# Rounded w_down blocks moved from w_up into w_o, and a new order of the first w_up products

## The chip, the cores and the metric

The kernel runs on one core of a Trainium2 chip. The metric is the device time of one execution in microseconds (us), the median of three runs. One execution was also taken with the hardware profiler; the profile's times are counted from the first instruction of that execution.

## The reference, cut to what matters

One encoder layer on 512 tokens of width 2048, all in float32: an attention and pooling part that ends in the product with `w_o`, a normalised residual, and a feed-forward part that ends in the product with `w_down`.

```python
m = concat(a, p) @ w_o                       # (512, 2048) @ (2048, 2048)
x = x + rms_norm(m, post_mix_g)
h = rms_norm(x, pre_ffn_g)
up = causal_dwconv(h @ w_up, conv_w, conv_b) # w_up: (2048, 2 * 5632), three taps along the tokens
y = (gelu(up[..., :5632]) * up[..., 5632:]) @ w_down
x = x + rms_norm(y, post_ffn_g)
```

## The kernel before, in words

**Arithmetic.** A float32 operand is split into a rounded part and the rest: ScalarE writes the rounded part (`L141`), VectorE subtracts it from the source (`L142`). A product is then rounded x rounded + rounded x rest + rest x rounded. The large products use a scheme with seven instead of eight half-size products (numbered 1 to 7), in which some factors are sums of blocks. Product 1 needs the weight block (0,0); the sums of products 5, 6 and 4 are made one from another, by adding further blocks to the same tile with a DMA that accumulates. Such DMAs are issued on GpSimd (`L1087` for w_up). Products 3 and 7 share a second tile in the same way, product 2 has a block of its own.

**Stages.** The order is: q, k, v and pooling projections and attention (to about 390 us), w_o with its seven products (to 548 us), the passage to w_up, w_up in 43 pairs of column blocks with seven products each and one plain block beforehand (to 1456 us), w_down in chunks, and the output.

**Order.** TensorE's instructions run in the order in which the program writes them. For the other engines a planner orders the instructions by estimated times, within the dependencies; each engine and each DMA queue (SP's and GpSimd's) then works its list in order, so that an instruction that waits holds everything listed behind it. A tile takes its place in memory when it is first used, in the group of buffers that its tag names, and gives it back after its last use.

**w_o.** `wo_product(i, cc)` runs one product on one column half, in four steps of one weight tile each. A step takes a tile that was loaded and rounded ahead (four tiles ahead rounded, two more loaded).

**The passage.** The last w_o product ends with tokens 256 to 511 not yet normalised. `norm`, `x2`, `keep_x` and `norm_x` make the new residual, and `hn` is its normalised form. `turn_back(2, pair, ...)` turns two of the sixteen column blocks of `hn` on TensorE (tile `xt`); ScalarE copies them out (`L989`), and after every second pair a quarter of `hT` (tile `gT`) is rounded. Eight such turns are needed. Products 1 and 2 need only tokens 0 to 255 and can run before them. The plain block (`up`, in four quarters, weights `w_0` to `w_3`) needs the turned tokens, and the other products need the sums of h that `h_sums` makes on VectorE and ScalarE (tiles `a` and `h`).

**w_up.** `Factors` holds the order of all products, loads raw weights ahead, and rounds them ahead: `get()` hands out the next and calls `prefetch`, which loads up to ten entries and rounds up to four ahead. Rounded weights lie in eight buffers (`w4`, two for each weight), raw ones in five (`raw4`) and in four more (`raw_x`). Pairs in `alone` use block (0,0) by itself for product 1 and load a new tile for the sum of product 5. The order starts with

```python
begin = [(k, i) for k in range(3) for i in (1, 2)] + [(0, 5), (3, 1), (0, 3), (3, 2), (0, 6)]
self.order[6:6] = [("w", q) for q in range(4)]
```

where `(k, i)` is product i of pair k and `("w", q)` a quarter of the plain block. Results of products 1, 6, 7 and 4 of one pair add up in one PSUM bank (`qa`), 5 and 3 in another (`qg`), 2 in a third (`qd`); `keep` copies them out.

**w_down's first chunk.** Its factors are prepared earlier. Sums of blocks are written to DRAM tiles `t5`, `t7`, `t6`, `t4` (`first_sum`), one step at a time, by `more_sums(1)`: a copy (`L302`, or `L305` on SP's queue late in the kernel) or an accumulation (`L309`, GpSimd). Three factors that need no sum (`READY`) are rounded ahead as six half blocks (`ready_parts`): each is loaded to `rw`, rounded to `rwh` and `rwl`, and both are stored to DRAM. Before the change these six stand as entries `(None, at)` in w_up's order, from entry 60 on, every 24 entries.

Of the kernel before, what the change touches and what calls it, by code (L numbers as in the profile page):

```python
# [9 lines left out]
F32 = mybir.dt.float32  # L10
# [5 lines left out]
P = 128  # L16
# [16 lines left out]
AHEAD = 3  # L33
READY_FROM, READY_EVERY = 60, 24
SCALE = 1.0 / math.sqrt(DH)
# [47 lines left out]
def encoder_layer(ctx: ExitStack, tc: tile.TileContext, x, xT, vecs, rel, post_mix, post_ffn,  # L83
# [121 lines left out]
    def g_tokens(gT, kb, t):  # L205
        return tuple(v[:, t % 2 * P:(t % 2 + 1) * P] for v in g_half(gT, kb, t // 2))

    def part(w, *idx):
        return tuple(v[(slice(None),) + idx] for v in w)
# [78 lines left out]

    first_sum = {i: [dram.tile([P, CU, S], F32, name=f"t{i}{cc}") for cc in range(2)] for i in (5, 7, 6, 4)}

    def sums_in_dram():
# [322 lines left out]
    with tc.tile_pool(name="p1", bufs=2, reuse_waits="tile") as p1:  # L614
# [215 lines left out]
        def wo_left(name, k, t, tiles=None):  # L830
# [7 lines left out]
            return parts  # L838

        wo_banks = [bank(f"m{n}") for n in range(8)]  # L840
        ONTO = 6, 3, 7, 4

        def wo_product(i, cc, left, between=None):
            at = 2 * cc + (4 if i in (2, 5, 3) else 0)
            ps = wo_banks[at:at + 2]
            for q in range(4):
                w = weights.get(f"wo{i}_{cc}_{q}")
                for j in range(2):
                    kb = 2 * q + j
                    for t in range(2):  # L850
                        mm3(ps[t], tuple(v[:, kb, t * P:(t + 1) * P] for v in left), part(w, j),
                            i not in ONTO and kb == 0, kb == 7, i in ONTO)
                if between:
                    between(q)
            return ps
# [18 lines left out]
    if True:  # L874
# [161 lines left out]
        class Factors:  # L1036
# [3 lines left out]
            def __init__(self):  # L1040
# [19 lines left out]
            def load(self, k, i):  # L1060
# [7 lines left out]
                if k is None:  # L1068
                    at, j = ready_parts[i]
                    v = self.raw[k, i] = raw4("rw")  # L1070
                    nc.sync.dma_start(v.rearrange("p (a b) -> p a b", a=2),
                                      first_block(at[0], at[1] - 1, 0)[:, 2 * j:2 * j + 2, :])
                elif i == 1 and (k, "w") not in self.raw:
                    raw("w" if k in self.alone else "x", raw4("wx") if k in self.alone[:4] else raw_x("wx"), 0, 0)
                elif i == 5 and k in self.alone[:4]:
                    raw("x", raw_x("wx") if k else raw4("wx"), 0, 0)
                    self.add(k, "x", 1, 0)
# [11 lines left out]
            def make(self, k, i):  # L1089
                if k == "w":  # L1090
                    weights.tiles.append(weights.made(*weights.loaded[len(weights.tiles)]))
                    self.made.append(None)
                    return
                if k is None:
                    at, j = ready_parts[i]
                    parts = w4("rwh"), w4("rwl")
                    split(*parts, self.raw[k, i])
                    for dest, v in zip(ready_w[at], parts):
                        nc.sync.dma_start(dest[:, 2 * j:2 * j + 2, :], f32(v).rearrange("p (a b) -> p a b", a=2))
                    self.made.append(None)  # L1100
                    return
# [24 lines left out]

            def get(self, n=AHEAD):
                while self.order[self.used][0] is None:
                    self.used += 1
# [93 lines left out]
    def first_right(cc, i, ring):  # L1223

        v = ring(f"t{i}")
        source = first_sum[i][cc] if i in first_sum else first_block(cc, *{2: (1, 0), 3: (1, 1)}[i])
# [66 lines left out]
    if True:  # L1293
# [6 lines left out]

        def parts_of(v, *sizes):

            ends = [sum(sizes[:i + 1]) for i in range(len(sizes))]
            return [v[:, e - n:e] for e, n in zip(ends, sizes)]

        held = {}

        def holder(name):
# [4 lines left out]
            return held[name]  # L1313

        def two(v):
            return v.rearrange("p (a b) -> p a b", a=2)

# [164 lines left out]
        gates[0] = gate(0, plain_z(ups))  # L1482
# [8 lines left out]

        for k, i in [at for at in factors.order[10:] if at[0] is not None]:
            seven(k, i)
# [261 lines left out]
```

## Time and profile before

| | us |
|---|---|
| median of 3 runs | 1902.74 |
| lowest and highest run | 1897.75, 1904.64 |
| the profiled execution | 1895.72 |
| its span, first to last instruction | 1893.8 |
| TensorE busy in the span | 1851.8 |
| TensorE busy in 412 to 548.2 (most of w_o) | 136.20 of 136.20 |
| TensorE busy in 550 to 700 | 127.75 of 150 |
| TensorE busy in 676.7 to 1456.2 (w_up) | 772.03 of 779.5 |

A row of a timeline gives the start, the duration, engine, line, operation, the tiles written and read, the shape and the count, and in brackets the idle time before it with what ended it. Matmuls of a row overlap: the distance between starts is what counts. A row of stages gives busy time for each engine, then the clock granted to TensorE (1.00 is full), the DMA engines' mean busy share and the rate in GB/s.

### The profile page before, as it was taken

What the parts mean: (1) busy time and instruction counts of PE and PEld (TensorE: products, weight loads), DVE (VectorE), ACT (ScalarE), POOL (GpSimd) and SP (SyncE); (2) the same over time, 40 slices, a digit from 0 to 9 for tenths busy, and PEclk for the clock granted to TensorE, in tenths of its full rate; (3) what the DMA queues carried; (4) which work ended last, traced back from release to release, by engine and by line L of the source; (5) the groups of instructions that cost most, each with busy time, mean ns of one, the idle gap of its engine ahead of it and who ended that gap; (6) DMA issues with size and microseconds to landing.
All of it is one profiled execution on the core that took longest, in us unless ns stands there. A gap on an engine that the chain in (4) does not pass through costs nothing.

```text
span 1893.8 us, 25400 instructions
## 1 busy us (share of the span) xinstructions
PE 1851.8 (98%) x9530; PEld 1586.0 (84%) x9530; DVE 1489.4 (79%) x1782; ACT 1105.6 (58%) x1449; POOL 310.1 (16%) x411
## 2 busy tenths in 40 slices
PE   9999999999997899999999999999999999999998
PEld 7888888888886788888888888888888788888886
DVE  6988778787676677877777877777776799899885
ACT  7655555465585556666656566665654665565553
POOL 3411001100001121221211221212121001111111
PEclk9999999999998999999999999999999999999999
DMA  8699987997687889999989998888888977877785
GB/s 315 179 317 298 311 248 222 272 266 250 220 294 188 186 188 208 230 231 225 206 217 224 222 217 202 200 203 205 206 176 251 357 236 179 210 199 171 177 232 156
DMA packets 139610, 430.73 MB, mean 227 GB/s; under 512 B 12064, under 2 KB 15520, under 8 KB 133792
## 3 DMA queue, kind: packets, MB, share of 16 engines
q0 software_dynamic: 56016, 177.75, 46.7%
q1 hardware_dynamic: 83472, 251.36, 37.9%
q8 instruction: 75, 1.23, 0.3%
q14 instruction: 47, 0.39, 0.1%
HBM read 375.07 MB, written 104.33 MB: 253 GB/s over the span
## 4 chain that ended last, share of the span: by engine, by line
PE 87%; DMA 6%; DVE 3%; issue 2%; ACT 1%; POOL 0%; SPq 0%; POOLq 0%; DVEq 0%; ACTq 0%
PE qa L171 16%; PE qa L177 9%; PE qg L171 8%; PE qg L177 4%; PE qd L171 4%; PE pa L163 4%; PE pa L165 4%; PE pa L166 4%; PE m L163 3%; PE m L166 3%; PE m L165 3%; PE qd L177 2%; PE pg L163 2%; PE pg L165 2%; PE pg L166 2%
## 5 line engine op out<-in xcount | busy, mean ns | idle before, releaser
L171 PE MATMUL qa<-gT,wfh 128*128 128x512 f32 x1200 | 302.1, 394 | 0.0
L142 DVE TENSOR_TENSOR wfl<-x,wfh 128x1024 fp32r<-128x1024 f32 x165 | 202.0, 1224 | 91.6 <-ACT wfh L141 83.4
L171 PEld LDWEIGHTS qa<-gT,wfh 128*128 128x128 f32 x1200 | 216.7, 190 | 39.0
L141 ACT ACTIVATE wfh<-x 128x1024 fp32r<-128x1024 f32 x165 | 174.4, 1057 | 111.0 <-PE qg L171 44.3
L1087 POOL DMA_DIRECT2D x<-in_w_up x125 | 107.5, 860 | 489.6 <-DVE wfl L142 459.8
L171 PE MATMUL qg<-h,wfh 128*128 128x512 f32 x688 | 174.1, 396 | 9.1 <-ACT m L1410 9.1
L177 PE MATMUL qa<-gT,wfl 128*128 128x256 f32 x1200 | 168.5, 283 | 10.3 <-ACT m L1415 7.6
L177 PEld LDWEIGHTS qa<-gT,wfl 128*128 128x128 f32 x1200 | 157.8, 191 | 16.6 <-ACT m L1415 9.2
L171 PEld LDWEIGHTS qg<-h,wfh 128*128 128x128 f32 x688 | 130.6, 191 | 38.9 <-ACT m L1410 11.9
L142 DVE TENSOR_TENSOR bl<-b,bh 128x2048 fp32r<-128x2048 f32 x56 | 127.2, 2287 | 18.6 <-ACT bh L141 11.7
L141 ACT ACTIVATE wfh<-wy 128x1024 fp32r<-128x1024 f32 x100 | 105.3, 1053 | 60.8 <-PE qd L171 39.9
L141 ACT ACTIVATE bh<-b 128x2048 fp32r<-128x2048 f32 x56 | 106.1, 1914 | 55.9 <-DVE b L1217 23.3
L142 DVE TENSOR_TENSOR wfl<-wy,wfh 128x1024 fp32r<-128x1024 f32 x100 | 121.9, 1219 | 13.5 <-ACT wfh L141 9.2
L163 PE MATMUL pa<-bh,ah 128*128 128x512 f32 x320 | 124.5, 389 | 0.0
L165 PE MATMUL pa<-bl,ah 128*128 128x512 f32 x320 | 124.5, 389 | 0.0
L166 PE MATMUL pa<-bh,al 128*128 128x512 f32 x320 | 124.5, 389 | 0.0
L177 PEld LDWEIGHTS qg<-h,wfl 128*128 128x128 f32 x688 | 95.0, 193 | 6.9
L171 PE MATMUL qd<-gT,wfh 128*128 128x512 f32 x400 | 99.6, 391 | 0.0
L177 PE MATMUL qg<-h,wfl 128*128 128x256 f32 x688 | 96.8, 284 | 0.0
L171 PEld LDWEIGHTS qd<-gT,wfh 128*128 128x128 f32 x400 | 75.3, 189 | 15.4
L171 PE MATMUL qa<-h,wfh 128*128 128x512 f32 x344 | 86.1, 392 | 0.0
L142 DVE TENSOR_TENSOR wfl<-wz,wfh 128x1024 fp32r<-128x1024 f32 x50 | 61.2, 1223 | 28.4 <-PE qa L171 22.4
(568 smaller groups left out, 4276.4 us busy)
## 6 DMA issues: line engine op xcount, KB each, us to landing
x<-in_w_up POOLq DMA_DIRECT2D x125, 512.0 KB, 6.5
b<-in_w_down SPq DMA_DIRECT2D x32, 1024.0 KB, 6.9
wt<-in_w_o POOLq DMA_DIRECT2D x24, 1024.0 KB, 15.3
wz<-in_w_up SPq DMA_DIRECT2D x43, 512.0 KB, 5.1
wy<-in_w_up SPq DMA_DIRECT2D x43, 512.0 KB, 4.7
x<-in_w_up SPq DMA_DIRECT2D x43, 512.0 KB, 5.4
wy<-in_w_up POOLq DMA_DIRECT2D x43, 512.0 KB, 6.5
sum<-part POOLq DMA_DIRECT2D x38, 512.0 KB, 7.0
```

Of the source, the lines that this page charges most:

```text
L141: rounded = nc.scalar.activation(hi, src, AF.Copy)
L142: rest = nc.vector.tensor_sub(lo, src, f32(hi))
L163: nc.tensor.matmul(ps, l[0], r[0], start=first, stop=False, skip_group_check=onto)
L165: nc.tensor.matmul(low, l[0], r[1], start=False, stop=False, skip_group_check=onto)
L166: nc.tensor.matmul(ps, l[1], r[0], start=False, stop=last, skip_group_check=onto)
L171: nc.tensor.matmul(ps, w[0][:, kb], pairs[kb][0], start=fresh and not kb, stop=last, skip_group_check=not fresh)
L177: nc.tensor.matmul(ps[:, sl], w[1][:, kb], pair[:, sl], start=False, stop=last, skip_group_check=not fresh)
L1087: nc.gpsimd.dma_start(self.raw[k, what], self.block(k, m, kh), accum_op=ALU.add)
```

## The change

- **Pair 0 is no longer in `alone`.** Its product-1 weight tile stays; the next block is added to it after its rounding, and product 5 uses it, without a load of its own.
- **The order begins** with products 1 and 2 of four pairs; the plain block's quarters follow, then (0,5) and (0,3). Of the eight turns, 0 and 1 come after the seventh product, 2 and 3 after the eighth, 4 and 5 after the plain block's first quarter, 6 and 7 after its second.
- **Run-ahead.** Up to that point three weights are rounded ahead instead of four, and twelve entries may be loaded instead of ten; the plain block's quarters run 2, 2, 3 and 4 ahead.
- **`t4` is no longer stored.** Its copies and accumulations, which `more_sums(1)` issued at four of the turns, are gone. When w_down's first chunk needs it, `first_right` loads `t6` and adds the block with an accumulating DMA on GpSimd.
- **The six rounded half blocks** are no longer in w_up's order. `ready_step`, called after each step of w_o's products other than product 1, loads block b in step 5b, rounds it in step 5b + 5 and stores it in step 5b + 6. They use the places `h5` and `h2` in turn instead of `raw4` and `w4`; the rest is written over the raw block. `y21`, declared earlier and first written after product 4, has the place `h2` too.

```diff
-    first_sum = {i: [...] for i in (5, 7, 6, 4)}
+    first_sum = {i: [...] for i in (5, 7, 6)}
...
-                            (add, 7, (0, 1)), (add, 6, (1, 1)), (copy, 4, 6), (add, 4, (1, 0))):
+                            (add, 7, (0, 1)), (add, 6, (1, 1))):
...
+        def ready_step():
+
+            n, step[0] = step[0], step[0] + 1
+            for b, (at, j) in enumerate(ready_parts):
+                begin = 5 * b
+                if n == begin:
+                    v, hi = parts_of(h8((5, 2)[b % 2], "rw"), 1024, 1024)
+                    ready_tiles[b] = v, hi.bitcast(F32R)
+                    nc.sync.dma_start(two(v), first_block(at[0], at[1] - 1, 0)[:, 2 * j:2 * j + 2, :])
+                elif n == begin + 5:
+                    v, hi = ready_tiles[b]
+                    split(hi, v.bitcast(F32R), v)
+                elif n == begin + 6:
+                    v, hi = ready_tiles.pop(b)
+                    for dest, part_ in zip(ready_w[at], (f32(hi), v)):
+                        nc.sync.dma_start(dest[:, 2 * j:2 * j + 2, :], two(part_))
...
+                if i != 1:
+                    ready_step()
...
-                self.alone, self.open = (0, 1, 2, 3, n - 1), False
+                self.alone, self.open = (1, 2, 3, n - 1), False
...
-                begin = [(k, i) for k in range(3) for i in (1, 2)] + [(0, 5), (3, 1), (0, 3), (3, 2), (0, 6)]
+                begin = [(k, i) for k in range(4) for i in (1, 2)] + [(0, 5), (0, 3)]
...
-                self.order[6:6] = [("w", q) for q in range(4)]
-                for at in range(len(ready_parts)):
-                    self.order.insert(READY_FROM + READY_EVERY * at, (None, at))
+                self.order[8:8] = [("w", q) for q in range(4)]
...
-                ahead = ahead if self.open else min(ahead, 10)
+                ahead = ahead if self.open else min(ahead, 12)
...
-                self.prefetch(n)
+                self.prefetch(self.AHEAD if self.open else self.AHEAD - 1)
...
+        if i == 4:
+            nc.gpsimd.dma_start(v, first_block(cc, 1, 0), accum_op=ALU.add)
...
-        for k, i in factors.order[:5]:
+        for k, i in factors.order[:7]:
             start(k, i)
-        for pair in range(4):
-            turn_back(2, pair, bank(f"xt{pair}"))
-            more_sums(1)
-        start(2, 2)
-        for pair in (4, 5):
-            turn_back(2, pair, bank(f"xt{pair}"))
+        turn(0, 1)
+        start(3, 2)
+        turn(2, 3)
         factors.open = True
...
-            if q == 1:
-                for pair in (6, 7):
-                    turn_back(2, pair, bank(f"xt{pair}"))
...
-            factors.prefetch(factors.AHEAD)
+            factors.prefetch((2, 2, 3, factors.AHEAD)[q])
...
+            if q < 2:
+                turn(4 + 2 * q, 5 + 2 * q)
```

More of the change, by code (lines that the diff above doesn't have):

```diff
@@ L33 @@
 AHEAD = 3
-READY_FROM, READY_EVERY = 60, 24
 SCALE = 1.0 / math.sqrt(DH)
@@ L206, in g_tokens, with parts_of, two @@
         return tuple(v[:, t % 2 * P:(t % 2 + 1) * P] for v in g_half(gT, kb, t // 2))
+    def parts_of(v, *sizes):
+        ends = [sum(sizes[:i + 1]) for i in range(len(sizes))]
+        return [v[:, e - n:e] for e, n in zip(ends, sizes)]
+    def two(v):
+        return v.rearrange("p (a b) -> p a b", a=2)
     def part(w, *idx):
@@ L285, in encoder_layer @@
     weights.limit = FIRST_PART
-    first_sum = {i: [dram.tile([P, CU, S], F32, name=f"t{i}{cc}") for cc in range(2)] for i in (5, 7, 6, 4)}
+    first_sum = {i: [dram.tile([P, CU, S], F32, name=f"t{i}{cc}") for cc in range(2)] for i in (5, 7, 6)}
     def sums_in_dram():
@@ L838, in wo_left @@
             return parts
+        ready_tiles, step = {}, [0]
+        def ready_step():
[13 more added lines that the diff above has]
+                        nc.sync.dma_start(dest[:, 2 * j:2 * j + 2, :], two(part_))
         wo_banks = [bank(f"m{n}") for n in range(8)]
@@ L1067, in load @@
                     return
[L1068 to L1076, printed above, removed]
+                if i == 1 and (k, "w") not in self.raw:
+                    raw("w" if k in self.alone else "x", raw4("wx") if k < 4 else raw_x("wx"), 0, 0)
+                elif i == 5 and k in self.alone[:3]:
+                    raw("x", raw_x("wx"), 0, 0)
                     self.add(k, "x", 1, 0)
@@ L1091, in make @@
                     weights.tiles.append(weights.made(*weights.loaded[len(weights.tiles)]))
[L1092 to L1099, printed above, removed]
                     self.made.append(None)
@@ L1125, in prefetch, with get @@
                     self.make(*self.order[len(self.made)])
-            def get(self, n=AHEAD):
-                while self.order[self.used][0] is None:
-                    self.used += 1
+            def get(self):
                 self.used += 1
                 self.prefetch(0)
-                self.prefetch(n)
+                self.prefetch(self.AHEAD if self.open else self.AHEAD - 1)
                 v, self.made[self.used - 1] = self.made[self.used - 1], None
@@ L1313, in holder @@
             return held[name]
-        def two(v):
-            return v.rearrange("p (a b) -> p a b", a=2)
         def new_z():
@@ L1457, in start, with turn @@
             keep(k, i)
-        for k, i in factors.order[:5]:
+        def turn(*which):
+            for pair in which:
+                turn_back(2, pair, bank(f"xt{pair}"))
+        for k, i in factors.order[:7]:
             start(k, i)
-        for pair in range(4):
-            turn_back(2, pair, bank(f"xt{pair}"))
-            more_sums(1)
-        start(2, 2)
-        for pair in (4, 5):
-            turn_back(2, pair, bank(f"xt{pair}"))
+        turn(0, 1)
+        start(3, 2)
+        turn(2, 3)
         factors.open = True
@@ L1490, in next_first @@
             firsts.append((firsts[0][0] if firsts else first_left(), r))
-        for k, i in [at for at in factors.order[10:] if at[0] is not None]:
+        for k, i in factors.order[12:]:
             seven(k, i)
```

5 lines of the change are left out of this document (1 added, 4 removed).

## The prediction

> **What bounds the kernel now.** I read the page's engine shares first, then busy time by stage, then TensorE's timeline where it is not full, and from there the timelines of ScalarE, GpSimd and VectorE.
>
> ```profile
> span 1893.8 us, 25400 instructions
> PE 1851.8 (98%) x9530; PEld 1586.0 (84%) x9530; DVE 1489.4 (79%) x1782; ACT 1105.6 (58%) x1449; POOL 310.1 (16%) x411
> ```
>
> TensorE is the bound, so only its idle or half-clocked time can be won. Busy time by stage (PE, PEld, DVE, ACT, POOL, then granted clock, DMA share, GB/s) shows where it is full:
>
> ```profile
> 500.00:548.20 48.20, 48.20 (x231) 40.21 (x230) 37.98 (x40) 39.37 (x61) 2.36 (x2) 1.00 0.72 256
> 676.70:1456.20 779.50, 772.03 (x4418) 679.82 (x4417) 604.02 (x759) 472.47 (x617) 164.37 (x198) 1.00 0.89 211
> ```
>
> w_o is full to its end and w_up has 7.5 us of holes. Between them lies the passage. For the ideal lengths I need three units from TensorE's timeline: a pair's seven products, a quarter of the plain block, a pair of transposes.
>
> ```profile
> 548.16 1.98 PE L171 MATMUL qa<-gT,wfh 128*128 128x512 f32 x8
> ...
> 577.99 1.04 PE L984 MATMUL xt<-ident,hn 128*128 128x128 f32 x8
> 578.78 0.48 PE L163 MATMUL up<-gT,w_1h 128*128 128x512 f32 x1
> 584.31 0.39 PE L163 MATMUL up<-gT,w_2h 128*128 128x512 f32 x1
> ...
> 676.70 2.00 PE L171 MATMUL qa<-gT,wfh 128*128 128x512 f32 x8
> 696.19 2.00 PE L171 MATMUL qa<-gT,wfh 128*128 128x512 f32 x8
> ```
>
> Seven products take 696.19 - 676.70 = 19.49 us, one 2.785; a quarter 5.53; one turn 0.79. From 548.16 to 676.70 the order holds 25 products, 4 quarters, 8 turns: 69.6 + 22.1 + 6.3 = 98.0 us of the 128.5, so **the passage loses 30.5 us**. From there to 1456.2, the end of the stage's row above, the other 276 of the 43 x 7 products need 768.5 of 779.5 us: **w_up loses 11.0 us**.
>
> **The passage's losses** (in brackets idle time and releaser):
>
> ```profile
> 564.84 0.33 PE L984 MATMUL xt<-ident,hn 128*128 128x128 f32 x1 [2.58 <-DVE hn L1150]
> 596.63 0.79 PE L163 MATMUL up<-gT,w_3h 128*128 128x512 f32 x1 [6.71 <-ACT gT L141]
> 606.00 1.98 PE L171 MATMUL qg<-h,wfh 128*128 128x512 f32 x8
> 615.55 3.78 PE L171 MATMUL qg<-h,wfh 128*128 128x512 f32 x8 [3.83 <-ACT m L1410]
> 623.57 1.12 PE L177 MATMUL qa<-h,wfl 128*128 128x256 f32 x8
> ```
>
> ScalarE and GpSimd show the cause of the large one, VectorE what follows:
>
> ```profile
> 572.78 1.55 ACT L989 ACTIVATE a<-xt,vec 128x256 f32<-128x256 f32 x4
> 592.17 1.06 ACT L141 ACTIVATE wfh<-wx 128x1024 fp32r<-128x1024 f32 x1 [16.75 <-DMA wx<-in_w_up]
> 569.59 1.19 POOL L309 DMA_DIRECT2D t<-in_w_down  x1 [5.59 <-DMA t<-t]
> 573.72 0.91 POOL L1087 DMA_DIRECT2D wx<-in_w_up  x1 [2.94 <-ACT a L989]
> 553.46 4.87 DVE L957 SCALAR_TENSOR_TENSOR x<-y,small,x 128x1024 f32<-128x1024 f32 x4
> 558.24 1.22 DVE L142 TENSOR_TENSOR wfl<-wz,wfh 128x1024 fp32r<-128x1024 f32 x1
> 564.03 2.74 DVE L1150 TENSOR_SCALAR hn<-x,small 128x1024 f32<-128x1024 f32 x4 [1.18 <-POOL small L971]
> 601.35 2.35 DVE L142 TENSOR_TENSOR h<-a,h 128x1024 fp32r<-128x1024 f32 x2
> 615.63 1.22 DVE L142 TENSOR_TENSOR h<-a,h 128x1024 fp32r<-128x1024 f32 x1
> ```
>
> ScalarE stands 16.75 us at the rounding of pair 0's product-5 weight, whose accumulating load was issued at 573.72 on GpSimd's queue, behind the 1 MB accumulation of 569.59; the copies of the last transposes and the sums' roundings are queued behind it on ScalarE. VectorE makes the last of h's roundings at 615.63, and product (0,3) at 615.55 runs into it.
>
> **Pair 0's weight kept, t4 not stored, order changed.** The change removes that load and rebuilds the sum right after product 1's rounding, at about 545, so it has landed long before ScalarE needs it. Two 1 MB copies on SP's queue and two 1 MB accumulations on GpSimd's queue leave the passage. From the fifth product's end (562.1) I lay out the new order with the units above: (2,2), (3,1) to 567.7; `hn` is complete at 566.8, so the first stall goes; turns 0, 1 to 569.3; (3,2) to 572.0; turns to 573.6; then quarters and turns to 598.9. The first quarter needs 1.55 + 1.06 + 1.22 us of ScalarE and VectorE after its turns, 573.1, just in time, and two PSUM banks while four pairs' accumulators are held: I charge 1 us. Before, the fourth quarter ended at 606.00 with (3,1) and (3,2) still to come: 7.1 + 5.6 - 1 = 11.7 us ahead.
>
> Now (0,5) and (0,3) follow directly, and the last turns end at 587.8 with only two quarters behind them. Their copies and rounding on ScalarE (1.55 + 1.06) end at 590.4, and after that VectorE has about 14 operations, 12 of gT and h and two weights, at 1.14 each (two took 2.35 at 601.35): done at 606.4. So (0,3) starts at about 606.5, waits some 4 us, costs 1.8 of half clock as before (3.78 against 1.98), and (0,6) starts at about 611 instead of 623.57: 12.5 us ahead. Behind it, the old order lost 53.1 - 15 x 2.785 = 11.3 us; that order stays, but pair 0's sum now has two products (5.6 us) instead of four between its fifth and sixth use, where rounding, GpSimd's issue and landing need some 9.7 (1.06 + 1.22 + 0.9 and the row below):
>
> ```profile
> x<-in_w_up POOLq DMA_DIRECT2D x125, 512.0 KB, 6.5
> ```
>
> That is 4 us short, partly hidden by the wait at (0,3); I charge 2.5. **Passage: -10 us**, between 0 (VectorE's sums end as late as before) and -22 (neither this nor the wait at (0,3) shows, and most of the 11.3 goes). The kept weight holds one of the five `raw` buffers until (0,4), so the plain block's second load waits for (2,2)'s rounding (558.24 + 1.22); 6.5 of landing and 2.3 of rounding bring it to 568.3, and its quarter comes at 580.7: nothing, unless that rounding slips by 12 us. The shorter run-ahead (three made instead of four) costs nothing at 2.785 us a product against 2.3 of rounding; uncovered it would cost one rounding, 2.3.
>
> **Rounded blocks out of w_up.** Each of the last five of the six is followed by a stall:
>
> ```profile
> 828.38 1.22 PE L177 MATMUL qa<-gT,wfl 128*128 128x256 f32 x8 [0.97 <-ACT m L1419]
> 902.40 1.22 PE L177 MATMUL qa<-gT,wfl 128*128 128x256 f32 x8 [1.35 <-ACT m L1415]
> 971.89 3.50 PE L171 MATMUL qg<-h,wfh 128*128 128x512 f32 x8 [2.39 <-ACT m L1410]
> 1044.59 1.22 PE L177 MATMUL qa<-gT,wfl 128*128 128x256 f32 x8 [1.24 <-ACT m L1415]
> 1093.54 2.11 PE L171 MATMUL qg<-h,wfh 128*128 128x512 f32 x8 [1.35 <-ACT m L1410]
> ```
>
> The tile of the rounded rest and its stores:
>
> ```profile
> L142 DVE TENSOR_TENSOR rwl<-rw,rwh x6: 1216/1226/1226, 756.4 to 1084.2; 128x1024 fp32r<-128x1024 f32 x6
> DMA to landing us min/median/max: 3.8/6.4/6.8
> ```
>
> The blocks take two of the eight `w4` tiles and keep them until a store has landed. The idle sums to 7.3 us, and 971.89 ran 1.5 long at a lower clock. I take **-9**, between -7 and -11.
>
> The Trainium skill ("TensorE: Matmul & The Clock Gate", Part 1) says that the clock falls only after an idle window of about 3.4 us. By that rule no stall here loses clock, and this term would be -7.3; the row at 971.89 lost clock after 2.39 us, so the row decides.
>
> **The blocks in w_o.** Six loads of 0.5 MB, six roundings, twelve stores of 0.5 MB go on SP's queue between the loads of w_o. They spread over 31 steps of twelve matmuls, half a quarter or 2.77 us each: 9.4 MB in 86 us, 110 GB/s on top of what the first three rows show. The fourth row is the most that was moved with TensorE full:
>
> ```profile
> 424.00:436.00 12.00, 12.00 (x55) 9.94 (x54) 11.34 (x13) 5.62 (x6) 0.00 (x0) 1.00 0.70 231
> 448.00:460.00 12.00, 12.00 (x55) 9.94 (x54) 7.05 (x6) 5.37 (x7) 0.00 (x0) 1.00 0.97 332
> 480.00:500.00 20.00, 20.00 (x90) 16.57 (x89) 11.78 (x11) 9.56 (x13) 0.00 (x0) 1.00 0.64 197
> 1480.00:1500.00 20.00, 20.00 (x90) 16.57 (x89) 19.01 (x14) 16.96 (x18) 1.46 (x2) 1.00 1.02 394
> ```
>
> A store is issued a step after its rounding, so SP hardly waits. With 110 more, two rows stay under 394 and the 12 us at 448 would ask for 442, some 1.5 us late, less than the step by which six weights run ahead. Only VectorE at 424-436 (11.34 of 12) is tight; two roundings (2.46) fall into 424-448. Cost 0, with +5 as the far end, if VectorE's 2.5 us and as much of half clock surface.
>
> **t4 made on the way in.** The two last first-chunk weights now need a load and a 1 MB accumulation on GpSimd. The two loads issued between 1488 and 1500 land in 8.0 us in the middle, so by about 1500 and 1505; the first is rounded later:
>
> ```profile
> t<-t SPq DMA_DIRECT2D x2, 1024.0 KB, 8.0
> 1511.80 1.90 ACT L141 ACTIVATE bh<-t 128x2048 fp32r<-128x2048 f32 x1
> ```
>
> Some 11 us lie between. An accumulation of half the size takes 6.5, so 13 for this one, 2 to 4 late; products run three behind roundings, 16 us, so I take 0, up to +4 if ScalarE's wait holds its copies.
>
> **Sum:** -10 - 9 + 0 + 0 = -19 us, span 1875. The profiled execution took 1895.72 us (span plus 1.9), 7 below the median 1902.74. From the median: **1884 us**.
>
> **Rivals.** (a) The stall only moves: ScalarE is held by another sum, (0,6)'s, with h's roundings behind it, and (0,3) starts no earlier in the order than now. For: the 5.6 us distance. Against: 1 MB accumulations no longer stand ahead of it. Passage 0, 1894 us, half of it inside 0.5%. (b) w_o does not hold the blocks and gives back w_up's 9 us: 1893. Against: 394 GB/s above. (c) More: passage -22: 1872. (d) Slower: the second buffer set lies in the place of `y21`, declared earlier. If that place is taken at the declaration, not at the first write, blocks 1, 3, 5 are made only after `y21`'s last read (553.46 + 4.87 = 558.3), each 6.4 + 2.3 + 6.4 = 15.1 us for load, rounding and stores, one after another, to 603.6; the first turns can then be copied to that place 34 us late: +34 - 10 - 9 = +15, 1918 us. It decides from two such blocks on. Against: the eight PSUM banks of w_o are named before `pm3` gets one, and `pm3`'s products run without waiting. (e) Several parts do nothing, 1900.
>
> **Chances.** Forecast 0.60 (1873 to 1892), (a) 0.17, (b) 0.07, (c) 0.07, (d) 0.05, (e) 0.04. 0.5%, about what a measurement tells from no change, is 9.5 us, down to 1893. Faster 0.77: the forecast with (c) and half of (a) and (b), less 0.02; slower 0.08: (d) and noise in (e); same 0.15. Range 1866 to 1900.
>
> **What would show it.** Right: no `t` in the passage; ScalarE's longest wait there under 6 us; `xt` without 2.58; (0,6) some 12 us earlier; `rwl` between 425 and 505 and no hole from 720 to 1400; w_o still 100%. Wrong: `rwl` after 548; idle TensorE before 548; or a wait over 8 us at `qg<-h`.

## The result, and the profile after

| us | before | after |
|---|---|---|
| median | 1901.03 (4 runs, 1897.75 to 1904.64) | 1882.36 (4 runs, 1881.14 to 1884.60) |
| the profiled execution | 1895.72 | 1881.14 |
| its span | 1893.8 | 1879.3 |

The ratio is 0.9903, with a 95% interval of 0.988 to 0.9925: **faster by about 1%**. The medians are 18.7 us apart and the two profiled executions 14.6, because the one of before lies 5 us below its median and the one of after 1 us below. Where the time went can only be read from the profiled executions, and the pieces below add up to their difference.

The engine shares of the kernel after, then its busy time by stage (the columns are those of the prediction's stages):

```profile
span 1879.3 us, 25378 instructions
...
PE 1846.3 (98%) x9530; PEld 1582.3 (84%) x9530; DVE 1488.1 (79%) x1782; ACT 1104.6 (59%) x1449; POOL 310.4 (17%) x411
```

```profile
390.00:549.20 159.20, 158.93 (x717) 131.61 (x716) 122.99 (x124) 106.60 (x141) 3.28 (x3) 1.00 0.88 304
549.20:665.50 116.30, 101.26 (x529) 85.18 (x529) 87.02 (x103) 70.46 (x102) 16.87 (x20) 0.94 0.76 192
665.50:1434.20 768.70, 768.70 (x4419) 678.98 (x4418) 597.94 (x753) 467.45 (x611) 164.37 (x198) 1.00 0.88 201
1434.20:1480.00 45.80, 43.43 (x184) 35.25 (x183) 33.00 (x26) 28.57 (x28) 3.85 (x6) 0.96 0.97 386
1480.00:1520.00 40.00, 35.22 (x146) 28.64 (x145) 25.43 (x19) 15.90 (x16) 4.99 (x7) 0.91 0.96 289
```

In four pieces of the span, each with what was predicted for it:

| us | before | after | difference | predicted |
|---|---|---|---|---|
| to the end of w_o | 548.2 | 549.2 | +1 | 0 |
| passage | 128.5 | 116.3 | -12.3 | -10 |
| w_up | 779.5 | 768.7 | -10.9 | -9 |
| w_down and the end | 437.5 | 445.1 | **+7.6** | 0 |

(The differences are taken from the starts of the first instructions, to a hundredth.) w_up is what the prediction called its ideal length, with TensorE busy in all of it. In w_o, with the blocks in it, TensorE was idle for 0.27 us. The passage won a little more than forecast. One piece went the other way: w_down lost 7.6 us, and the last row of stages shows where: 4.78 us of idle TensorE in 40 and a clock of 0.91. In the kernel before the same place, 22 us later in time, was full:

```profile
1500.00:1540.00 40.00, 40.00 (x179) 33.10 (x178) 33.47 (x23) 20.75 (x21) 4.28 (x6) 1.00 0.78 275
```

In the passage, TensorE's timeline of the kernel after shows two larger waits left: 6.47 us for VectorE's sums of h, and 4.18 us later on for a PSUM bank that ScalarE copies out. ScalarE's longest wait there is 4.29 us, for a later pair's weight, where it was 16.75:

```profile
549.25 1.98 PE L170 MATMUL qa<-gT,wfh 128*128 128x512 f32 x8
...
609.26 3.56 PE L170 MATMUL qg<-h,wfh 128*128 128x512 f32 x8 [6.47 <-DVE h L141]
...
613.62 1.12 PE L176 MATMUL qa<-h,wfl 128*128 128x256 f32 x8
...
652.17 2.07 PE L176 MATMUL qa<-gT,wfl 128*128 128x256 f32 x8 [4.18 <-ACT m L1420]
...
665.53 2.00 PE L170 MATMUL qa<-gT,wfh 128*128 128x512 f32 x8
```

```profile
625.28 1.06 ACT L140 ACTIVATE wfh<-wy 128x1024 fp32r<-128x1024 f32 x1 [4.29 <-DMA wy<-in_w_up]
```

In w_down, three timelines of the kernel after, GpSimd's, ScalarE's and TensorE's, tell one story:

```profile
1478.75 1.31 POOL L1241 DMA_DIRECT2D t<-in_w_down  x1 [10.82 <-DMA t<-t]
1481.42 1.29 POOL L1241 DMA_DIRECT2D t<-in_w_down  x1 [1.35 <-DMA t<-t]
```

```profile
1495.54 1.92 ACT L140 ACTIVATE bh<-t 128x2048 fp32r<-128x2048 f32 x1 [2.50 <-DMA t<-in_w_down]
1505.54 1.91 ACT L140 ACTIVATE bh<-t 128x2048 fp32r<-128x2048 f32 x1 [8.09 <-DMA t<-in_w_down]
...
1508.31 1.06 ACT L1271 ACTIVATE part<-pa 128x512 f32<-128x512 f32 x2
```

```profile
1508.94 0.80 PE L162 MATMUL pa<-bh,ah 128*128 128x512 f32 x1 [4.78 <-ACT part L1271]
```

The two 1 MB accumulations that now make `t4` are issued at 1478.75 and 1481.42. ScalarE can round their tiles at 1495.54 and 1505.54, so they took 16.8 and 24.1 us. ScalarE stands 8.09 us at the second, and the copy `part<-pa`, which frees the PSUM bank for TensorE's next product, is listed behind it. TensorE waits 4.78 us, and its first matmul afterwards takes 0.80 us where such a matmul takes 0.39 at full clock (the `up` row of the prediction). The first eleven matmuls took 4.75 us from start to start in place of 2.5: for that stretch the clock was about halved.

This wait is longer than the 3.4 us that the Trainium skill ("TensorE: Matmul & The Clock Gate", Part 1) asks for before the clock falls, so this row agrees with it; a shorter one, further down, does not.

### The profile page after: what moved, and what is told of

The parts are those of the page before. It is cut to its first block, busy times and chain, and to the rows that moved or that the text cites. A ratio compares the mean times of both kernels' runs of the same rounds, so it can differ in the third digit from the quotient of the medians.

```text
span 1879.3 us, 25378 instructions
## 1 busy us (share of the span) xinstructions
PE 1846.3 (98%) x9530; PEld 1582.3 (84%) x9530; DVE 1488.1 (79%) x1782; ACT 1104.6 (59%) x1449; POOL 310.4 (17%) x411
## 4 chain that ended last, share of the span: by engine, by line
PE 62%; DMA 3%; DVE 3%; issue 2%; ACT 1%; POOL 0%; POOLq 0%; DVEq 0%; ACTq 0%; SPq 0%
PE qa L170 16%; PE qa L176 8%; PE qg L170 8%; PE qg L176 4%; PE qd L170 4%; PE pa L162 3%; PE pa L164 3%; PE pa L165 3%; PE qd L176 2%; PE pg L162 2%; PE pg L164 2%; PE pg L165 2%; DMA t<-in_w_down 1%; PE pd L164 1%; PE pd L165 1%
```

## The experiments

The first theory: the passage gained because the first pair's accumulating load no longer stands behind `t4`'s accumulations and because the new order fills VectorE's time; `t4` on the way in costs w_down its 7.6 us. The rivals: the order alone, what left the queues alone, or the places where the blocks now lie. The passage is measured from the first product 1 to the start of (4,1), w_down from its first product to the span's end. "Old order" and "new order" stand for the sequence of products and turns together with the run-ahead that goes with it; no run separates these. The median of before, measured beside each of these kernels, was 1899.75 to 1901.87 us.

### t4 stored again, its transfers in w_o

```diff
+            if n in (32, 33, 36, 38):
+                more_sums(1)
...
-        if i == 4:
-            nc.gpsimd.dma_start(v, first_block(cc, 1, 0), accum_op=ALU.add)
```

> The changed kernel, but the fourth sum t4 of w_down is written to DRAM again, its two copies and two accumulations issued in w_o at the steps 32, 33, 36 and 38, after the last rounded block; w_down then only loads it. Theory A (the two 1 MB accumulations on the way in, which landed 16.7 and 24.0 us after their issue, hold ScalarE at bh<-t, and ScalarE's late part<-pa holds TensorE 4.8 us and halves its clock for a moment): the stage from the first product of w_down to the end falls from 445.2 us to 437.5 to 440, TensorE's wait of 4.8 us at pa is gone, and the run is 5 to 8 us shorter than the changed kernel, 1874 to 1878. Theory B (w_down is longer for another reason, such as the end of the kernel or the clock): 443 to 446 us for that stage and 1880 to 1884 in all. Theory C (the moved transfers collide in w_o with its own loads or with y21): w_down gains as in A, but w_o or the passage grows by 3 to 6 us, 1879 to 1883.

Measured: 1882.58 us, ratio 0.9904 (0.9875 to 0.9932). The stages of this run, the end of w_o and w_down:

```profile
520.00:558.60 38.60, 33.23 (x149) 27.08 (x148) 22.45 (x20) 28.71 (x44) 0.93 (x1) 0.91 0.93 288
1443.80:1881.00 437.20, 426.82 (x1885) 353.10 (x1883) 366.40 (x277) 241.05 (x253) 48.46 (x49) 0.99 0.78 219
```

w_down is back at 437.5 us and its wait is gone: making `t4` on the way in is the whole of the 7.6 us. But w_o ends at 558.6, 9.4 us later, with 5.4 us of idle TensorE towards its end: theory C, at a higher price than it named. In w_o the four transfers cost 9.4 us, more than the 7.6 that w_down got back.

### The blocks back in w_up

```diff
-                if i != 1:
-                    ready_step()
...
+                for at in range(len(ready_parts)):
+                    self.order.insert(READY_FROM + READY_EVERY * at, (None, at))
```

> The changed kernel with the six blocks for w_down rounded in w_up again, at the places in its list of weights where they stood, and none in w_o. Theory A (w_up's 10.9 us are the blocks' alone, and w_o holds them for nothing): w_up grows from 768.7 to 778 to 780 us, w_o stays at 159 to 160 us, the run is 1890 to 1894. Theory B (a part of w_up's gain is the run-ahead that the passage leaves behind, and the holes in w_up would be shorter with it): w_up 771 to 775 us, 1884 to 1889. Theory C (the blocks cost w_o something that the loads' 2 us longer landing shows): w_o 2 to 4 us shorter as well, 1887 to 1890.

Measured: 1896.00 us, ratio 0.998 (0.9958 to 1.0003). Its w_o, passage and w_up:

```profile
393.50:552.20 158.70, 158.70 (x717) 131.73 (x716) 117.09 (x118) 102.26 (x135) 3.28 (x3) 1.00 0.74 246
...
552.20:667.70 115.50, 101.67 (x529) 85.67 (x528) 87.02 (x103) 70.43 (x102) 16.87 (x20) 0.96 0.78 193
667.70:1448.80 781.10, 772.16 (x4418) 679.78 (x4417) 603.31 (x759) 472.25 (x617) 164.31 (x198) 1.00 0.88 210
```

Theory A, with w_up and the run above its ranges by 1 and 2 us: w_up grows by 12.4 us and has its holes again, 158.7 us of w_o against 159.2 says that the blocks cost at most half a microsecond there, and the passage does not notice them. (w_o started 3.5 us late in this execution, after waits of 1.7 and 0.9 us in the attention part; why they came is not settled.)

### The old order of the passage

```diff
-                begin = [(k, i) for k in range(4) for i in (1, 2)] + [(0, 5), (0, 3)]
+                begin = [(k, i) for k in range(3) for i in (1, 2)] + [(0, 5), (3, 1), (0, 3), (3, 2), (0, 6)]
...
-                self.order[8:8] = [("w", q) for q in range(4)]
+                self.order[6:6] = [("w", q) for q in range(4)]
```

and the turns, the run-ahead of four and the limit of ten entries as in the kernel before.

> The changed kernel with the old order of the passage: products 1 and 2 of three pairs, (3,1) and (3,2) later, the transposes at their old places and the old run-ahead; the first pair's weight is still kept, t4 is still made on the way into w_down and the blocks still lie in w_o. Theory A (of the passage's 12.3 us the order makes most, because the fourth pair's two products fill the time in which VectorE makes the sums of h): passage 7 to 11 us longer than the changed kernel's 116.3, so 123 to 127, run 1889 to 1893. Theory B (what left the passage makes most: the load of 2 MB and the t4 transfers at the turns): passage 118 to 121 us, run 1883 to 1887.

Measured: 1881.08 us, ratio 0.9903 (0.9865 to 0.9941). Its passage and w_down:

```profile
548.70:663.90 115.20, 103.24 (x529) 86.80 (x528) 86.93 (x103) 70.01 (x102) 16.86 (x20) 0.94 0.75 193
...
1432.60:1878.90 446.30, 429.08 (x1885) 354.23 (x1883) 366.33 (x277) 241.01 (x253) 51.17 (x51) 0.98 0.78 219
```

The old order is not slower: 115.2 us against 116.3, better than even theory B allowed. (The new order's passage took 115.5 and 115.8 us in the two runs above, which do not touch it, so a gap of 1 us is hardly more than these runs differ.) **The new order made none of the passage's gain**, and my first theory fell in this half. What left the passage made all of it. TensorE's timeline of this run, at (0,3) and (0,6):

```profile
601.78 2.37 PE L170 MATMUL qg<-h,wfh 128*128 128x512 f32 x8 [0.61 <-DVE zc L1311]
...
607.72 1.12 PE L176 MATMUL qa<-h,wfl 128*128 128x256 f32 x8
```

The first of h's sums on VectorE, here and in the changed kernel:

```profile
577.20 1.22 DVE L1381 TENSOR_TENSOR a<-a,a 128x1024 f32<-128x1024 f32 x1
```

```profile
585.62 1.22 DVE L1381 TENSOR_TENSOR a<-a,a 128x1024 f32<-128x1024 f32 x1
```

The later turns make h's sums start 8.4 us later. So the new order, though it runs the same products ahead of (0,6), comes to it 64.4 us after the first product and the old one after 59.0. The products behind (0,6) then wait more in the old order and take back all but 1.1 us.

### VectorE made slower

```diff
             for i in range(2):
+                for _ in range(2):
+                    nc.vector.tensor_tensor(halves[i][2], halves[i][2], halves[i][2], op=ALU.max)
+            for i in range(2):
                 split(*quarter(0, 1, i), halves[i][1])
```

> The changed kernel with four more VectorE instructions (a maximum of a tile with itself in place, about 1.14 us each, 4.6 us in all, no value changes) just ahead of the two splits of the sums that (0,3) and (0,6) read. Theory A (VectorE's chain of sums of h sets when (0,3) starts): (0,3) starts 4 to 5 us later, TensorE's wait there is 10.5 to 11.5 us in place of 6.5, the passage 4 to 5 us longer, with a cost of the clock perhaps 5 to 7; run 1886 to 1889. Theory B (something else, such as ScalarE's roundings of the weights or the transposes, sets it and VectorE is only the last by a hair): 0 to 1.5 us longer, run 1882 to 1884.

Measured: 1887.35 us, ratio 0.9925 (0.9896 to 0.9955). Its passage, and product (0,3) on TensorE's timeline:

```profile
548.50:670.80 122.30, 103.30 (x529) 86.80 (x529) 91.69 (x107) 70.59 (x102) 16.87 (x20) 0.92 0.72 182
```

```profile
611.33 3.79 PE L170 MATMUL qg<-h,wfh 128*128 128x512 f32 x8 [9.22 <-DVE h L141]
```

VectorE is busy 4.67 us longer (91.69 against 87.02), the wait at (0,3) is 2.75 us longer and the passage 6.0: nearer to A than to B. Only 2.75 of the 4.67 show at (0,3). The planner listed VectorE's work in another sequence here: a step of `zc` and a rounding of h, 1.8 us together, come behind the rounding that (0,3) waits for and stand ahead of it in the changed kernel, which fits the rest. With the new order VectorE's sums do set the start of (0,3); with the old one its wait is 0.61 us.

### t4's transfers meant for w_up

```diff
-        for k, i in factors.order[12:]:
+        for n, (k, i) in enumerate(factors.order[12:]):
+            if n in (60, 84, 108, 132):
+                more_sums(1)
             seven(k, i)
```

and the accumulation on the way in removed, as in the first run.

> The changed kernel, but t4 is written to DRAM again, by two 1 MB copies and two 1 MB accumulations issued one at a time amid w_up, before its products 60, 84, 108 and 132 of the list; w_down only loads it. Theory A (w_up, with a share of 0.86 to 0.90 for the DMA engines and no idle TensorE, takes four transfers so far apart for nothing): w_down to the end falls to 437 to 438 us as it did with t4 in w_o, w_up stays at 768.7 to 770, run 1872 to 1876. Theory B (each 1 MB transfer holds back the 512 KB loads and accumulations of w_up as the rounded blocks did, about 1.6 us of hole for each block before): w_up 774 to 776, run 1878 to 1882.

Measured: 1883.73 us, ratio 0.9915 (0.9886 to 0.9944). Its passage and w_down, and a row of SP's queue:

```profile
548.40:673.70 125.30, 103.83 (x529) 87.41 (x528) 87.25 (x103) 70.47 (x102) 19.31 (x22) 0.90 0.83 212
...
1442.40:1880.00 437.60, 426.77 (x1885) 353.07 (x1883) 366.13 (x277) 241.27 (x253) 48.44 (x49) 0.99 0.77 218
```

```profile
573.84 0.63 SPq L312 DMA_DIRECT2D t<-t  x1
```

The edit did not do what was meant. It places the transfers in w_up, but nothing in the program held them there, and the planner issued the copies at 573.84 and 576.87, in the passage, and the accumulations behind them. Neither theory was tried; whether w_up takes them for nothing stays open. What the run does show is that the passage of the new order pays 9.0 us for them.

### Old order, t4's transfers at the turns

What is left of the change here is the kept weight and the blocks in w_o.

```diff
         def turn(*which):
             for pair in which:
                 turn_back(2, pair, bank(f"xt{pair}"))
+                if which == (0, 1, 2, 3):
+                    more_sums(1)
```

> The run with the old order of the passage, and also with t4's two copies and two accumulations back at the first four transposes. What is left of the change is the kept weight of the first pair and the blocks in w_o. Theory A (of the 12 to 13 us that the passage lost, t4's transfers make most, because they stand in the queues ahead of the pairs' weights): passage 121 to 127 us in place of the 115.2 of the old order without them; w_down to the end 437 to 438; run 1877 to 1884. Theory B (the kept weight, 1 MB less to load, makes most): passage 115 to 118; run 1870 to 1874.

Measured: **1870.91 us** (1869.59 to 1873.53), ratio 0.9848 (0.9813 to 0.9882), the fastest of all. Its stages from w_o to the end:

```profile
390.30:549.00 158.70, 158.70 (x718) 131.70 (x717) 122.72 (x123) 107.33 (x141) 3.28 (x3) 1.00 0.88 305
...
549.00:664.00 115.00, 103.47 (x529) 87.16 (x528) 86.94 (x103) 70.13 (x102) 19.25 (x22) 0.94 0.90 231
664.00:1434.40 770.40, 768.98 (x4418) 678.86 (x4417) 598.05 (x753) 468.79 (x611) 164.44 (x198) 1.00 0.87 201
1434.40:1871.70 437.30, 426.41 (x1885) 352.89 (x1883) 366.30 (x277) 241.43 (x253) 48.88 (x49) 0.99 0.77 218
```

With the kept weight, `t4`'s transfers are free in the passage (115.1 against 115.2 us without them), and w_down has its 437.3 us. GpSimd's queue fits this: the first pair's accumulation is issued 25 us ahead of `t4`'s, at 546.40.

```profile
546.40 0.93 POOL L1108 DMA_DIRECT2D wx<-in_w_up  x1 [28.25 <-DVE wfl L141]
...
571.39 1.21 POOL L316 DMA_DIRECT2D t<-in_w_down  x1 [6.91 <-DMA t<-t]
```

### Old order, first pair loaded anew, t4 not in the passage

```diff
-                self.alone, self.open = (1, 2, 3, n - 1), False
+                self.alone, self.open = (0, 1, 2, 3, n - 1), False
...
-                elif i == 5 and k in self.alone[:3]:
-                    raw("x", raw_x("wx"), 0, 0)
+                elif i == 5 and k in self.alone[:4]:
+                    raw("x", raw_x("wx") if k else raw4("wx"), 0, 0)
```

> The run with the old order of the passage, but the first pair's weight is loaded anew for its sum, as before the change. What is left of the change is t4 made on the way into w_down and the blocks in w_o. Theory A (t4's transfers make most of the passage's gain): passage 115 to 118 us, w_down to the end 445 to 446, run 1881 to 1884. Theory B (the kept weight makes most): passage 121 to 127, run 1887 to 1893.

Measured: 1879.64 us, ratio 0.9892 (0.9858 to 0.9926). Its passage, and the landing of the accumulation in question (KB each, then us from issue to landing):

```profile
549.30:663.70 114.40, 102.89 (x529) 87.38 (x528) 86.95 (x103) 70.30 (x102) 17.77 (x21) 0.94 0.78 196
```

```profile
wx<-in_w_up POOLq DMA_DIRECT2D x1, 512.0 KB, 5.8
```

The order and the run-ahead are the old ones, as in the two runs before. Without the kept weight the passage is as short, as long as `t4`'s transfers are away. The two runs together show that neither removal "makes most" of the gain: **each alone is enough**, and the second gains nothing more.

### New order, t4's transfers at the turns

```diff
                 turn_back(2, pair, bank(f"xt{pair}"))
+                more_sums(1)
```

> The changed kernel with its new order, and t4's two copies and two accumulations at the first four transposes, in the middle of the passage. Theory A (the new order, whose eight products need their weights early and whose transposes come later, is indifferent to them): passage 116 to 118 us, w_down to the end 437 to 438, run 1873 to 1876, better than the change. Theory B (the transfers cost the same in either order): passage 122 to 128, run 1879 to 1885.

Measured: 1881.07 us, ratio 0.9908 (0.9875 to 0.9942). Its passage, and where ScalarE and then TensorE stand:

```profile
548.70:671.30 122.60, 103.78 (x529) 87.25 (x528) 87.14 (x103) 70.53 (x102) 19.24 (x22) 0.90 0.84 216
```

```profile
599.40 1.06 ACT L140 ACTIVATE wfh<-wx 128x1024 fp32r<-128x1024 f32 x1 [6.72 <-DMA wx<-in_w_up]
```

```profile
606.32 2.07 PE L170 MATMUL qg<-h,wfh 128*128 128x512 f32 x4 [6.57 <-DVE h L141]
```

Theory B: 6.3 us more than without them. In the new order (0,3) and (0,6) follow (0,5) directly. ScalarE comes to the next sum of the first pair at 592.68 (599.40 - 6.72), while its accumulation lies behind `t4`'s two; the roundings of h's sums are listed behind it, and TensorE waits 6.57 us for them in (0,5). In the old order the same accumulation landed 15.1 us after its issue at 581.47, at 596.6 and so nearly as late as here, but ScalarE only came to it at 599.61 and did not wait:

```profile
599.61 1.05 ACT L140 ACTIVATE wfh<-wx 128x1024 fp32r<-128x1024 f32 x1
```

### The kernel before with the blocks in w_o alone

```diff
-                for at in range(len(ready_parts)):
-                    self.order.insert(READY_FROM + READY_EVERY * at, (None, at))
...
+                if i != 1:
+                    ready_step()
```

> The kernel before with one part of the change: the six blocks for w_down rounded in w_o and not in w_up. The passage is all as before: old order, the first pair's weight loaded anew, t4's transfers at the first four transposes. Theory A (the passage's 12 us come from a meeting of two things: the first pair's reload is put into the queues behind t4's transfers; either of them alone is free, as the three runs with one or none of them show with 114.5 to 115.2 us): passage 127 to 130 us, ScalarE waits 15 us or more for wx, w_up 768.7 to 770, run 1883 to 1887. Theory B (the passage was long because of the blocks, or of what the change declares elsewhere): passage 115 to 118, run 1871 to 1875.

Measured: 1886.41 us, ratio 0.9925 (0.9895 to 0.9955). Its passage and w_up, ScalarE's wait, and the accumulation that it waits for:

```profile
548.60:677.20 128.60, 106.33 (x529) 88.65 (x528) 87.14 (x103) 70.27 (x102) 20.15 (x23) 0.91 0.83 207
677.20:1446.80 769.60, 769.02 (x4419) 678.84 (x4418) 597.89 (x753) 467.12 (x611) 164.57 (x198) 1.00 0.88 201
```

```profile
592.96 1.06 ACT L141 ACTIVATE wfh<-wx 128x1024 fp32r<-128x1024 f32 x1 [17.36 <-DMA wx<-in_w_up]
```

```profile
wx<-in_w_up POOLq DMA_DIRECT2D x1, 512.0 KB, 19.7
```

Theory A: the passage is as long as before, and w_up is short. The blocks have nothing to do with the passage's gain.

### The same, with t4's accumulations behind the first pair's

```diff
             def add(self, k, what, m, kh):
-                nc.gpsimd.dma_start(self.raw[k, what], self.block(k, m, kh), accum_op=ALU.add)
+                ins = nc.gpsimd.dma_start(self.raw[k, what], self.block(k, m, kh), accum_op=ALU.add).ins
+                more_sums.behind = more_sums.behind or ins
...
-            with tc.issue_after(pace()) if more_sums.paced else nullcontext():
+            with tc.issue_after(pace() if more_sums.paced else more_sums.behind):
...
-            more_sums(1)
+            if pair < 2:
+                more_sums(1)
...
+            if q == 1:
+                more_sums(2)
```

> The run before it in this list (old passage, blocks in w_o), but t4's two accumulations are put into GpSimd's queue behind the accumulation of the first pair's reload in place of ahead of it; the two copies stay at the first two transposes. Nothing leaves the passage. Theory A (the place in GpSimd's queue makes it: the reload's accumulation, issued at 573.7 in the kernel before, landed at 592.1 behind two accumulations of 1 MB): it lands before 582, and the passage is 115 to 119 us; w_down to the end 437 to 438; run 1870 to 1875. Theory B (the sum of what is moved makes it, in whatever order): passage 124 to 130, run 1880 to 1887.

Measured: 1874.01 us, ratio 0.9861 (0.9837 to 0.9886). Its passage, and its accumulations about the place:

```profile
548.50:665.30 116.80, 103.16 (x530) 87.36 (x529) 87.09 (x103) 70.58 (x102) 20.16 (x23) 0.94 0.89 228
```

```profile
t<-in_w_down POOLq DMA_DIRECT2D x2, 1024.0 KB, 18.4
wx<-in_w_up POOLq DMA_DIRECT2D x1, 512.0 KB, 9.0
```

Nothing leaves the passage, nothing is loaded less, and it loses 11.8 us of its 128.6. The accumulation lands 9.0 us after its issue in place of 19.7. **The place in GpSimd's queue is the cause**; the amount of data can account for no more than the 2 us by which this passage exceeds the shortest ones.

### The new order alone

```diff
-                self.alone, self.open = (1, 2, 3, n - 1), False
+                self.alone, self.open = (0, 1, 2, 3, n - 1), False
```

on top of the new order with `t4` at the turns.

> The changed kernel with its new order, but the first pair's weight loaded anew for its sum and t4's transfers at the first four transposes: of the change in the passage only the order is left. Theory A (the order helps by itself, as the prediction has it): passage 118 to 122 us, less than the old passage's 128.5, run 1875 to 1880. Theory B (the order gains nothing, and what it reads early makes it more open to late accumulations, as it was with t4's transfers alone, 122.7 us): passage 124 to 130, run 1880 to 1888.

Measured: 1889.03 us, ratio 0.9936 (0.9913 to 0.9958). Its passage:

```profile
549.30:681.10 131.80, 105.43 (x529) 88.54 (x528) 87.12 (x103) 70.38 (x102) 20.10 (x23) 0.88 0.80 202
```

At 131.9 us it is above theory B's range, and so is the run: the passage is 3.2 us worse than the old order's with the same load.

### The passage in all its forms

| passage, us (blocks in w_o) | old order | new order |
|---|---|---|
| first pair loaded anew, t4 at the turns | 128.6 | 131.9 |
| first pair loaded anew, t4's accumulations behind it | 116.8 | not run |
| first pair loaded anew, t4 not there | 114.5 | not run |
| first pair kept, t4 at the turns | **115.1** | 122.7 |
| first pair kept, t4 not there | 115.2 | 116.3 (the change) |

In every pair the old order is the shorter, in the last row by hardly more than the runs differ. And "t4 not there" costs w_down 7 to 9 us each time (445.1 to 446.3 against 437.3 to 437.7). So the best of these kernels keeps the first pair's weight and moves the blocks, and does not touch the order or `t4`: 1870.91 us against 1882.36, with no overlap between their runs. Each was measured beside its own runs of before, and the two ratio intervals just touch at 0.988, since the runs of before beside the better one spread from 1889 to 1910 us.

## Why the prediction was right or wrong

**The time.** 1884 against 1882.36. On the profiled execution the forecast was -19 and the result -14.6: two terms came out 2 us better each, one 7.6 us worse, w_o 1 us worse. The medians moved by 18.7 because the profiled execution of before lay 5 us below its median. That the median landed within 2 us is therefore partly luck; the terms of the sum did not all hold.

**t4 made on the way in: the step that failed.** I took 13 us for the 1 MB accumulation, twice that of half the size, found it "2 to 4 late", and priced that at 0 because products run three behind roundings. It took 16.8 and 24.1 us, and the second cost ScalarE 8.09 us. The far end named the right mechanism (ScalarE's wait holds its copies) with +4; it measured +7.6, of which 4.8 are the wait and 2.3 the slower matmuls behind it. The three products of slack do not help, because what TensorE lacked was not a rounded weight but a PSUM bank, whose copy stands in the same list of ScalarE. Doubling 6.5 us was not needed: the kernel before had accumulations of this very size in its passage, and 18.9 less the 11 us that I found between landing and rounding is some 8 us late, about the 8.09 that ScalarE waited.

```profile
t<-in_w_down POOLq DMA_DIRECT2D x2, 1024.0 KB, 18.9
```

**The cause in the passage: right.** ScalarE's 16.75 us came from an accumulation behind a 1 MB accumulation on GpSimd's queue, as the prediction read it; the run in which only the place of `t4`'s accumulations changed shows it. The prediction did not say that either removal would do alone.

**The order: wrong, and hidden by a good sum.** The prediction priced the kept weight, `t4`'s leaving and the order as one laid-out sequence, and the layout came out well. The passage began 1.1 us later than in the kernel before; counted from the first product, (0,5) was to start at 50.7 us and started at 49.9, (0,3) at 58.3 and started at 60.0, since VectorE's sums ended later than laid out, and (0,6) was to be 12.5 us ahead and was 11.0 (75.4 before, 64.4 after). Behind (0,6) I charged 2.5 us for the short distance to the first pair's next sum; the 15 products took 51.9 us in place of 53.1, so nothing was lost there. That is 3.7 us better than charged and, less the 1.5 us lost ahead of (0,6), makes the -12.3 in place of -10. But the layout was never made for the old order without the stall. That one gives 115.2. The second step that failed is "Now (0,5) and (0,3) follow directly": it counts (3,1) and (3,2) as won, and asks when h's sums end with the later turns, but not how much earlier they end with the turns where they were. With `t4` in the passage and (0,6) close behind (0,3), the new order also loses to a late accumulation what the old one does not (122.7 against 115.1).

**Blocks out of w_up: right, a little small.** -9 forecast, -10.9 with w_up at its ideal; moved alone they gave 9.9 (779.5 to 769.6), put back alone they cost 12.4. **Blocks in w_o: right.** 0, measured 0 to 0.5; w_o with them ran 158.7 of 158.7 us busy in the fastest kernel, at 305 GB/s.

**The rivals.** (a) did not come, but its mechanism is real: with `t4` in the passage, (0,6)'s sum held ScalarE 6.72 us. (b) and (d) fell, with w_o full but for 0.27 us and the blocks rounded between 425 and 490, as the tile's row of the kernel after has it:

```profile
L141 DVE TENSOR_TENSOR rw<-rw x6: 1218/1226/1227, 425.5 to 488.5; 128x1024 fp32r<-128x1024 f32 x6
```

(c) was not reached: it asked for a passage of 106.5 us, and the shortest in the table is 114.5, which is still 16.5 above the 98.0 of the prediction's ideal. (e), that parts do nothing, was true of two parts: the order, and `t4`'s leaving beside the kept weight.

**The signs.** No `t` in the passage, ScalarE's longest wait 4.29 us, under 6, `xt` without its wait, no hole in w_up, a wait of 6.47 us at `qg<-h`, under 8: as written, with (0,6) 11 us earlier in place of some 12 and 0.27 us of idle time in w_o. None of them could tell the order's share from the rest, and none looked at w_down.

## What to carry to other kernels

Where a change has several parts against one stall, lay out each part alone on the old kernel too: here two parts each removed the whole stall, a third cost time, and one good sum hid it. Before taking out a transfer that holds a small urgent one back, look at its place in the queue; here, putting it behind the urgent one won 11.8 of the 13.5 us by which the kept weight shortened the passage, and nothing had to leave. Work that is made "on the way in" has its latency in the list of the engine that reads it, and everything behind it in that list pays, here a copy that frees a PSUM bank. Price a transfer by one of its own size in the trace where there is one.

## What the runs showed of the hardware

An accumulating load of 512 KB on GpSimd's queue took 5.8 us with nothing large ahead of it, 9.0 with two 1 MB accumulations issued right behind it, and 19.7 behind them. GpSimd itself went on (the two issues at 1478.75 and 1481.42 are 2.7 us apart, and the first of these transfers took 16.8); the transfers landed in the sequence of their issue. The Trainium skill ("DMA: Bandwidth & Descriptors", Two DMAs through the same engine are not ordered) says that within one queue of one DMA engine descriptors start in order, and that a later one may complete before an earlier one has finished writing. The views here give issue and landing, not the start of descriptors; in these runs, what was put behind also landed behind.

A 1 MB accumulation took 16.8 and 24.1 us in w_down, where 289 to 386 GB/s were moved, two to three times the 8.0 us of the plain 1 MB loads at that place in the kernel before.

The clock can fall after less idle time than the 4.78 us at `t4`. In the fastest run TensorE waited 2.60 us in w_down, the matmul behind it took twice the 0.39 us of one at full clock, and the next ones followed each other after 0.43 us in place of 0.23:

```profile
1448.36 0.79 PE L164 MATMUL pd<-bl,ah 128*128 128x512 f32 x1 [2.60 <-DMA bl<-rw02l]
```

Like the prediction's row at 971.89, it lost clock after less than the 3.4 us of the Trainium skill ("TensorE: Matmul & The Clock Gate", Part 1).
